# Four of seven Strassen products of a feed-forward layer accumulate in one PSUM bank, and the first tap of its convolution moves from VectorE to ScalarE

## The chip, the cores and the metric

One Trainium2 chip, one core. The metric is the device time of one execution in microseconds (us). The engines are named as the profile names them: PE is TensorE (PEld its weight loads), DVE is VectorE, ACT is ScalarE, POOL is GpSimd, SP is SyncE, whose queue issues the transfers. PE writes its sums to PSUM, which has eight banks; all other tiles lie in SBUF.

## The reference, cut to what matters

The program is a four-layer encoder over 528 tokens (16 of them fixed) of width 1024, in fp32. Each layer is a mixer (attention, RWKV, RG-LRU, attention), a layer norm, a gated feed-forward layer with a convolution over time, and a layer norm. Only the feed-forward layer is touched:

```python
def _dw_conv(x, w, b, pad_left):
    y = lax.conv_general_dilated(x, w[:, None, :], window_strides=(1,), ...)
    return y + b

def _conv_glu_ffn(x, w_in, conv_w, conv_b, w_out):
    g, u = jnp.split(x @ w_in, 2, axis=-1)          # w_in: 1024 x 5632
    g = _dw_conv(g, conv_w, conv_b, FFN_CONV_LEFT)  # 3 taps per channel
    return (jax.nn.silu(g) * u) @ w_out             # w_out: 2816 x 1024

for i in range(DEPTH):                              # 4 layers
    m = mixer_of_layer_i(h)
    h = _layer_norm(DN_ALPHA * h + m, ln_g[i, 0], ln_b[i, 0])
    f = _conv_glu_ffn(h, ffn_w_in[i], ffn_conv_w[i], ffn_conv_b[i], ffn_w_out[i])
    h = _layer_norm(DN_ALPHA * h + f, ln_g[i, 1], ln_b[i, 1])
```

## The kernel before

**Precision.** An fp32 matrix product is made of three matmuls on rounded parts: weight and operand are each split into a high part (`whi`, `xhi`; an ACT cast) and a rest (`wlo`, `xlo`; a DVE subtraction), and `mm3` adds hi*hi, hi*lo and lo*hi in one PSUM bank. A DVE split of a weight tile reads the raw weight and the high part and writes `wlo` (line 577, and line 411 for weights that are not Strassen's).

**Tiling.** `ffn` works through the 2816 channels in 11 steps `i` of 256 channels; each step has kind 0 (the gate g) and kind 1 (u). Step 0 is done with ordinary products. In steps 1 to 10 each (step, kind), called a *key* below, is a 2x2 block product by Strassen and Winograd's scheme: seven *products*, numbered 1 to 7, each of 12 matmuls of 264 columns (4 slices of the contraction times `mm3`), in place of eight. `products` makes the weight operands: it loads two raw tiles (`wraw`, `wraw2`), lets POOL form their sums (lines 586 to 591), and casts and splits the results in four pairs: for products 1 and 2, then 5 and 6, then 7 and 4, then 3. The operands of the activations (`thi`, `tlo`) are made once per layer by `operand_sums`.

**Combination.** `product(key, p)` runs one product into a bank of its own and then adds it to the outputs `c11`, `c12`, `c21`, `c22` (halves of two tiles `gp`) and to a helper tile `pu`. It runs the products in the order 1, 2, 6, 5, 7, 4, 3; product 1 is copied by ACT (line 642), and the rest take seven DVE adds (line 640).

**After a key.** For kind 0, each of the two `gp` tiles goes through the convolution: two POOL memsets of the edge columns, the first tap with the bias on DVE (line 696), two more taps on DVE (line 699), then Silu on ACT (line 701). For kind 1 DVE multiplies (line 705), and ACT and DVE split the result into `phi` and `plo` (lines 416, 417). From step 3 on, one *partial product* with `w_out` follows most keys (`partial`, 36 matmuls for three steps' channels, two DVE adds to `h` at line 511); its weights are split at line 411.

**Order.** The kernel's text gives each engine its work; a scheduler then fixes one static order per engine at build time, and an engine runs its own list strictly in that order. Buffers are few: four `whi` and four `wlo` tiles, three `wraw`, two `wraw2`, three `pu`, four `gp`, eight banks. The feed-forward layers are alike, so the program runs the stretch described here four times.

Of the kernel before, what the change touches and what calls it, by code (L numbers as in the profile page):

```python
# [11 lines left out]
AF = mybir.ActivationFunctionType  # L12
ALU = mybir.AluOpType
# [6 lines left out]
T = META + SEQ  # L20
HT = T // 2
# [7 lines left out]
KF = D_FF // 128  # L29
# [34 lines left out]
class Params:  # L64
# [6 lines left out]
    def add(self, name, size):  # L71
        self.at[name] = (self.n, size // 128)
        self.n += size // 128
# [252 lines left out]
class Kern:  # L326
# [89 lines left out]
        nc.scalar.copy(hi, src)  # L416
        nc.vector.tensor_tensor(out=lo, in0=src, in1=hi.bitcast(F32), op=ALU.subtract)

    def mm3(self, out, w, ws, x, xs, start, stop):

        nc = self.nc
        nc.tensor.matmul(out, lhsT=w[0][ws], rhs=x[0][xs], start=start, stop=False)  # L422
        nc.tensor.matmul(out, lhsT=w[0][ws], rhs=x[1][xs], start=False, stop=False)  # L423
        nc.tensor.matmul(out, lhsT=w[1][ws], rhs=x[0][xs], start=False, stop=stop)  # L424

    def lin(self, ps, pieces, x, halves):

# [166 lines left out]
    def ffn(self, l, split=True):  # L594
        nc, a = self.nc, self.a
        with ExitStack() as es:
            self.banks()
            fp = es.enter_context(self.tc.tile_pool(reuse_waits="tile", name=f"ffn{l}", bufs=1))
            K2 = KD // 2
# [21 lines left out]
            def begin(key):  # L621
                if key not in live:
                    L = live[key] = dict(gen=self.products(a["ffn_in"][l, key[0] * 2 + key[1]], 512, fp))
                    L["w"] = next(L["gen"])
                    L["t"] = [fp.tile([128, T + 2], F32, name="gp", tag="gp", bufs=4) for _ in range(2)]
                    L["c"] = [[t[:, 1 + j * HT:1 + j * HT + HT] for j in range(2)] for t in L["t"]]
                    L["u"] = [fp.tile([128, HT], F32, name="pu", tag="pu", bufs=3) for _ in range(2)]
                return live[key]

            def product(key, p):  # L630

                L = begin(key)
                if p not in L["w"]:
                    L["w"].update(next(L["gen"]))
                ps = self.bank()[:, :HT]
                for k in range(K2):
                    self.mm3(ps, L["w"][p], (slice(None), slice(k * 128, k * 128 + 128)), pairs[p], (slice(None), k), k == 0, k == K2 - 1)
                (c11, c12), (c21, c22) = L["c"]
                p1, u = L["u"]
                add = lambda out, x: nc.vector.tensor_tensor(out=out, in0=x, in1=ps, op=ALU.add)  # L640
                if p == 1:
                    nc.scalar.copy(p1, ps)
                elif p == 2:
                    add(c11, p1)
                elif p == 6:
                    add(c12, p1)
                elif p == 5:
                    add(u, c12)
                elif p == 7:
                    add(c21, c12)  # L650
                    add(c22, u)
                elif p == 4:
                    add(c21, c21)
                else:
                    add(c12, u)


# [8 lines left out]
                        self.late_apply() if q else self.late_stats()  # L666
            begin((1, 0))
            operand_sums()
            slots, queue = [], []

            def pieces(m, ch):
# [7 lines left out]
            for i in range(KF // 2):  # L679
                cs = []  # L680
                for kind in (0, 1):
                    key = (i, kind)
                    if i:
                        for p in (1, 2, 6, 5, 7, 4, 3):
                            product(key, p)
                        dst = live.pop(key)["t"]
                    else:
                        dst = first[kind]
                    for j in range(2):
                        f = 2 * i + j  # L690
                        if kind == 0:
# [1 line left out]
                            nc.gpsimd.memset(gp[:, 0:1], 0.0)  # L693
                            nc.gpsimd.memset(gp[:, T + 1:T + 2], 0.0)
                            c = fp.tile([128, T], F32, name="cv", tag="cv", bufs=2)
                            nc.vector.tensor_scalar(out=c, in0=gp[:, 0:T], scalar1=self.p(f"fc_w{l}0", f),
                                                    scalar2=self.p(f"fc_b{l}", f), op0=ALU.mult, op1=ALU.add)
                            for q in (1, 2):
                                nc.vector.scalar_tensor_tensor(out=c, in0=gp[:, q:q + T], scalar=self.p(f"fc_w{l}{q}", f), in1=c,  # L699
                                                               op0=ALU.mult, op1=ALU.add)  # L700
# [1204 lines left out]
```

## Time and profile before

| | |
|---|---|
| time of three runs, median (lowest, highest) | 3550.47 us (3542.97, 3557.28) |
| the profiled execution's own time | 3547.82 us |
| its span | 3546.0 us |
| mean granted PE clock | 0.966 of full speed |
| busy share of the span | PE 91%, PEld 87%, DVE 79%, ACT 45%, POOL 28% |
| chain of work that ended last | PE 59%, DVE 22%, ACT 8%, issue 5%, POOL 3%, DMA 2% |

A busy share says how long an engine had an instruction in it. A PE that is shown busy is not at its peak, since matmuls are pipelined and their ends are modelled. The chain is the work followed back from the last instruction, at each step to what released it. Where a stretch of one layer is shown, it is that of the first layer unless the line says otherwise; times are from the start of the span.

### The profile page before, as it was taken

The page shows a single profiled execution, that of the slowest core. Times are in us where ns is not written, and L with a number is a line of the kernel's source. Part 1 is how long each engine was busy: PE and PEld are TensorE (multiplying, and loading weights), DVE is VectorE, ACT ScalarE, POOL GpSimd, SP SyncE. Part 2 cuts the span into 40 slices and gives each one's busy share as a digit, 9 for nine tenths or more (in the row PEclk, how much of TensorE's full clock was granted, in tenths as well). Part 3 has the DMA queues.
Part 4 walks back from the last instruction along what each step waited for, and adds up shares of the span by engine and source line. Part 5 has one row for each costly group of instructions (what it writes and reads, how often), then busy time and mean ns, then how long its engine had stood idle before and what let it go on. Part 6 is the DMA issues. An engine that isn't in the chain of part 4 may idle for free.

```text
span 3546.0 us, 77810 instructions
## 1 busy us (share of the span) xinstructions
PE 3229.4 (91%) x31961; PEld 3099.3 (87%) x31961; DVE 2799.9 (79%) x5158; ACT 1610.5 (45%) x3035; POOL 1003.2 (28%) x1438
## 2 busy tenths in 40 slices
PE   5999889997988888878899988989999899989998
PEld 5899889996977877868899988979999799979998
DVE  5877799979436767657999779789997787789997
ACT  4765444333333333324333468643334666543433
POOL 0000253323006455434533200045431000045341
PEclk9999999998989999989999989999999999999999
DMA  2011213322422112122233222213332011212332
GB/s 82 22 40 38 75 63 103 103 84 86 136 77 48 35 38 45 25 53 88 82 105 97 87 72 72 79 54 100 98 94 81 20 37 34 66 43 93 103 92 71
DMA packets 155557, 250.06 MB, mean 71 GB/s; under 512 B 78496, under 2 KB 85824, under 8 KB 154944
## 3 DMA queue, kind: packets, MB, share of 16 engines
q1 hardware_dynamic: 155200, 245.08, 22.7%
q8 instruction: 251, 4.11, 0.5%
q14 instruction: 106, 0.87, 0.1%
HBM read 227.93 MB, written 17.10 MB: 69 GB/s over the span
## 4 chain that ended last, share of the span: by engine, by line
PE 59%; DVE 22%; ACT 8%; issue 5%; POOL 3%; DMA 2%; SPq 0%; DVEq 0%; ACTq 0%; POOLq 0%
PE bank L424 13%; PE bank L422 13%; PE bank L423 13%; PE pj L218 8%; PE ps L218 3%; DVE wlo L577 3%; PE s L218 3%; PE ch L218 1%; ACT wv L218 1%; PE rb L218 1%; DVE cv L699 1%; DVE pst L218 1%; DVE gp L640 1%; DVE cv L705 1%; DVE wlo L411 1%
## 5 line engine op out<-in xcount | busy, mean ns | idle before, releaser
L422 PE MATMUL bank<-xhi,whi 128*128 128x264 f32 x2144 | 608.3, 289 | 38.6 <-ACT xhi L416 28.9
L423 PE MATMUL bank<-xlo,whi 128*128 128x264 f32 x2144 | 618.3, 290 | 23.7 <-DVE xlo L564 12.5
L424 PE MATMUL bank<-xhi,wlo 128*128 128x264 f32 x2144 | 613.0, 289 | 23.4 <-DVE wlo L577 21.6
L422 PEld LDWEIGHTS bank<-xhi,whi 128*128 128x128 f32 x2144 | 406.3, 192 | 41.2 <-ACT xhi L416 28.8
L423 PEld LDWEIGHTS bank<-xlo,whi 128*128 128x128 f32 x2144 | 410.4, 191 | 33.1 <-DVE xlo L564 17.8
L424 PEld LDWEIGHTS bank<-xhi,wlo 128*128 128x128 f32 x2144 | 409.4, 192 | 29.7 <-DVE wlo L577 27.2
L424 PE MATMUL bank<-phi,wlo 128*128 128x264 f32 x1408 | 401.2, 285 | 2.1 <-DVE wlo L411 2.1
L422 PE MATMUL bank<-phi,whi 128*128 128x264 f32 x1408 | 400.5, 284 | 0.0
L423 PE MATMUL bank<-plo,whi 128*128 128x264 f32 x1408 | 400.3, 284 | 0.0
L576 ACT CAST whi<-wraw 128x1024 fp32r<-128x1024 f32 (+1 forms) x240 | 217.3, 907 | 263.9 <-PE bank L423 164.4
L577 DVE TENSOR_TENSOR wlo<-wraw,whi 128x1024 fp32r<-128x1024 f32 (+1 forms) x240 | 321.3, 1340 | 10.5 <-ACT whi L576 10.0
L411 DVE TENSOR_TENSOR wlo<-wraw,whi 128x1024 fp32r<-128x1024 f32 (+1 forms) x218 | 243.7, 1118 | 105.1 <-ACT whi L410 102.3
L410 ACT CAST whi<-wraw 128x1024 fp32r<-128x1024 f32 (+1 forms) x218 | 205.6, 946 | 198.8 <-PE bank L423 140.6
L424 PE MATMUL bank<-thi,wlo 128*128 128x264 f32 x960 | 276.2, 288 | 21.3 <-DVE wlo L577 21.3
L423 PE MATMUL bank<-tlo,whi 128*128 128x264 f32 x960 | 274.7, 286 | 0.0
L422 PE MATMUL bank<-thi,whi 128*128 128x264 f32 x960 | 273.9, 286 | 0.0
L424 PEld LDWEIGHTS bank<-phi,wlo 128*128 128x128 f32 x1408 | 264.8, 188 | 2.8 <-DVE wlo L411 2.8
L422 PEld LDWEIGHTS bank<-phi,whi 128*128 128x128 f32 x1408 | 265.1, 188 | 0.0
L423 PEld LDWEIGHTS bank<-plo,whi 128*128 128x128 f32 x1408 | 264.7, 188 | 0.0
L591 POOL TENSOR_TENSOR wraw<-wraw,wsum 128x512 f32<-128x512 f32 x80 | 113.4, 1418 | 384.7 <-DVE wlo L577 313.1
L424 PEld LDWEIGHTS bank<-thi,wlo 128*128 128x128 f32 x960 | 182.6, 190 | 23.8 <-DVE wlo L577 23.8
L422 PEld LDWEIGHTS bank<-thi,whi 128*128 128x128 f32 x960 | 182.9, 191 | 0.0
(402 smaller groups left out, 9841.1 us busy)
## 6 DMA issues: line engine op xcount, KB each, us to landing
wraw<-in_ffn_in_dram SPq DMA_DIRECT2D x176, 512.0 KB
wraw<-in_ffn_out_dram SPq DMA_DIRECT2D x96, 384.0 KB
wraw<-in_mla_o_dram SPq DMA_DIRECT2D x48, 256.0 KB
wraw<-in_rw_rkv_dram SPq DMA_DIRECT2D x24, 512.0 KB
wraw<-in_lru_in_dram SPq DMA_DIRECT2D x20, 512.0 KB
wraw<-in_mla_q_dram SPq DMA_DIRECT2D x16, 512.0 KB
wraw<-in_ffn_out_dram SPq DMA_DIRECT2D x16, 512.0 KB
rkv<-ro SPq DMA_DIRECT2D x24, 264.0 KB
```

The costliest lines, as they stand in the source:

```text
L218: op.fn(*op.args, **op.kw)
L410: nc.scalar.copy(hi[:, :cols], raw[:, :cols])
L411: nc.vector.tensor_tensor(out=lo[:, :cols], in0=raw[:, :cols], in1=hi[:, :cols].bitcast(F32), op=ALU.subtract)
L422: nc.tensor.matmul(out, lhsT=w[0][ws], rhs=x[0][xs], start=start, stop=False)
L423: nc.tensor.matmul(out, lhsT=w[0][ws], rhs=x[1][xs], start=False, stop=False)
L424: nc.tensor.matmul(out, lhsT=w[1][ws], rhs=x[0][xs], start=False, stop=stop)
L576: nc.scalar.copy(hi[:, cut], x[:, cut])
L577: nc.vector.tensor_tensor(out=lo[:, cut], in0=x[:, cut], in1=hi[:, cut].bitcast(F32), op=ALU.subtract)
L591: e.tensor_tensor(out=a1[:, 1], in0=a1[:, 1], in1=s[:, 1], op=ALU.subtract)
L640: add = lambda out, x: nc.vector.tensor_tensor(out=out, in0=x, in1=ps, op=ALU.add)
L699: nc.vector.scalar_tensor_tensor(out=c, in0=gp[:, q:q + T], scalar=self.p(f"fc_w{l}{q}", f), in1=c, op0=ALU.mult, op1=ALU.add)
L705: nc.vector.tensor_tensor(out=c, in0=c, in1=dst[j][:, 1:T + 1], op=ALU.mult)
```

## The change

Products 6, 7 and 4 accumulate in the bank in which product 1 of their key stands, and product 3 in the bank of product 5. Between them ACT copies the running sum out: after 6 to the helper tile `u` (products 1+6), after 7 to `c22` (1+6+7), after 4 to `c21` (1+6+7+4). DVE adds three times: `c11` = product 2 + copy of product 1, `c22` += bank of product 5, `c12` = bank of products 5+3 + `u`. So a key has three DVE adds and four ACT copies, where it had seven and one. Product 1 of the next key runs between products 7 and 4 of the present one, and its weights are prepared that much earlier. The convolution's first tap, with scale and bias per channel, is an ACT activation. The number of matmuls is the same.

```diff
-    def mm3(self, out, w, ws, x, xs, start, stop):
+    def mm3(self, out, w, ws, x, xs, start, stop, more=False):
...
-                ps = self.bank()[:, :HT]
+                if p in (1, 2, 5):
+                    L[p] = self.bank()[:, :HT]
+                on = {6: 1, 7: 1, 4: 1, 3: 5}.get(p, p)
+                ps = L[on]
                 for k in range(K2):
-                    self.mm3(ps, L["w"][p], (slice(None), slice(k * 128, k * 128 + 128)), pairs[p], (slice(None), k), k == 0, k == K2 - 1)
+                    self.mm3(ps, L["w"][p], (slice(None), slice(k * 128, k * 128 + 128)), pairs[p], (slice(None), k),
+                             k == 0 and on == p, k == K2 - 1, True)
...
                 elif p == 6:
-                    add(c12, p1)
-                elif p == 5:
-                    add(u, c12)
+                    nc.scalar.copy(u, ps)
                 elif p == 7:
-                    add(c21, c12)
-                    add(c22, u)
+                    nc.scalar.copy(c22, ps)
+                    nc.vector.tensor_tensor(out=c22, in0=c22, in1=L[5], op=ALU.add)
                 elif p == 4:
-                    add(c21, c21)
-                else:
+                    nc.scalar.copy(c21, ps)
+                elif p == 3:
                     add(c12, u)
...
             begin((1, 0))
             operand_sums()
+            product((1, 0), 1)
...
                     if i:
-                        for p in (1, 2, 6, 5, 7, 4, 3):
+                        for p in (2, 6, 5, 7):
+                            product(key, p)
+                        nxt = (i, 1) if kind == 0 else (i + 1, 0)
+                        if nxt[0] < KF // 2:
+                            product(nxt, 1)
+                        for p in (4, 3):
                             product(key, p)
...
-                            nc.vector.tensor_scalar(out=c, in0=gp[:, 0:T], scalar1=self.p(f"fc_w{l}0", f),
-                                                    scalar2=self.p(f"fc_b{l}", f), op0=ALU.mult, op1=ALU.add)
+                            nc.scalar.activation(out=c, in_=gp[:, 0:T], func=AF.Identity, scale=self.p(f"fc_w{l}0", f), bias=self.p(f"fc_b{l}", f))
```

What the change does to the engines' lists is shown at two places of the first layer. Numbers in names tell tiles apart and differ between the two programs.

**DVE, the second key (step 1, kind 1).** Line 640 is an add before; lines 645 and 654 are adds after; line 577 is a weight split. Before:

```order
L640 TENSOR_TENSOR gp_5364<-pu_5366,bank_5405 128x264
L577 TENSOR_TENSOR wlo_5497<-wraw_5494,whi_5496 128x1024
L640 TENSOR_TENSOR pu_5367<-gp_5364,bank_5419 128x264
L577 TENSOR_TENSOR wlo_5538<-wsum_5533,whi_5537 128x1024
L640 TENSOR_TENSOR gp_5365<-gp_5364,bank_5438 128x264
L640 TENSOR_TENSOR gp_5365<-pu_5367,bank_5438 128x264
L640 TENSOR_TENSOR gp_5365<-gp_5365,bank_5453 128x264
L577 TENSOR_TENSOR wlo_5571<-wraw2_5532,whi_5570 128x1024
L640 TENSOR_TENSOR gp_5364<-pu_5367,bank_5472 128x264
```

And in the changed kernel:

```order
L645 TENSOR_TENSOR gp_5314<-pu_5316,bank_5377 128x264
L577 TENSOR_TENSOR wlo_5484<-wraw_5308,whi_5483 128x512
L577 TENSOR_TENSOR wlo_5528<-wsum_5523,whi_5527 128x1024
L654 TENSOR_TENSOR gp_5315<-gp_5315,bank_5413 128x264
L577 TENSOR_TENSOR wlo_5559<-wraw2_5522,whi_5558 128x1024
L645 TENSOR_TENSOR gp_5314<-pu_5317,bank_5413 128x264
```

The last two adds read the bank of product 5 (`bank_5413`): line 654 before product 3 may add to it, line 645 after. One split stands between them.

**ACT, between product 4 of a kind-0 key and product 6 of the next (step 4 in the changed kernel, and the corresponding place of the program before).** Line 701 before and 709 after is Silu; line 576 a cast of Strassen weights, line 410 one of `w_out`; line 642 the copy of product 1. Before:

```order
L576 CAST whi_6440<-wraw_6330 128x512
L701 ACTIVATE cv_6272<-cv_6272 128x528
L701 ACTIVATE cv_6279<-cv_6279 128x528
L642 COPY pu_6338<-bank_6340 128x264
L410 CAST whi_6467<-wraw_6466 128x768
```

And in the changed kernel, where line 656 copies product 4's sum, 705 is the first tap and 651 the copy of product 6's sum:

```order
L576 CAST whi_6338<-wsum_6334 128x1024
L656 COPY gp_6034<-bank_6037 128x264
L576 CAST whi_6369<-wraw2_6333 128x1024
L705 ACTIVATE cv_6261<-gp_6033,par_64 128x528
L705 ACTIVATE cv_6268<-gp_6034,par_64 128x528
L709 ACTIVATE cv_6261<-cv_6261 128x528
L576 CAST whi_6389<-wraw_6387 128x1024
L709 ACTIVATE cv_6268<-cv_6268 128x528
L576 CAST whi_6425<-wraw_6204 128x512
L651 COPY pu_6213<-bank_6214 128x264
```

The last row is now followed by PE: product 7 adds to `bank_6214` and so comes after the copy. Ahead of it stand both Silus, which follow three and four DVE taps.

## Rows read from the trace of the kernel before

**Rows 1.** The page's busy times by engine: us (share of the span) xinstructions.

```profile
PE 3229.4 (91%) x31961; PEld 3099.3 (87%) x31961; DVE 2799.9 (79%) x5158; ACT 1610.5 (45%) x3035; POOL 1003.2 (28%) x1438
```

**Rows 2.** Busy time in stretches of layer 1 (three rows) and layer 3.

```profile
core 0: us, PE busy (x) PEld busy (x) DVE busy (x) ACT busy (x) POOL busy (x), PEclk, DMA share, GB/s
468.00:536.00 68.00, 55.55 (x422) 53.26 (x420) 66.07 (x82) 29.43 (x42) 37.59 (x33) 0.97 0.23 74
536.00:563.00 27.00, 26.26 (x211) 25.85 (x212) 26.77 (x36) 10.53 (x16) 12.35 (x12) 1.00 0.24 74
563.00:776.00 213.00, 213.00 (x1750) 213.00 (x1750) 195.09 (x275) 83.03 (x111) 76.56 (x73) 1.00 0.32 99
2366.00:2434.00 68.00, 57.80 (x422) 56.15 (x423) 67.08 (x84) 29.52 (x41) 37.65 (x33) 0.92 0.23 74
```

**Rows 3.** PE's groups in 466 to 563 us; the last columns are idle us and releasers.

```profile
L424 PE MATMUL bank<-xhi,wlo 128*128 128x264 f32 x114 | 33.2, 295 | 6.0 <-DVE wlo L577 6.0
...
L422 PE MATMUL bank<-xhi,whi 128*128 128x264 f32 x113 | 32.6, 289 | 0.8 <-ACT whi L576 0.8
L424 PE MATMUL bank<-thi,wlo 128*128 128x264 f32 x79 | 23.0, 293 | 5.3 <-DVE wlo L577 5.3
...
L424 PE MATMUL bank<-phi,wlo 128*128 128x264 f32 x24 | 6.9, 289 | 1.0 <-DVE wlo L411 1.0
```

**Rows 4.** The order of time on DVE in the first layer: start us, us.

```profile
473.48 0.56 DVE L696 TENSOR_SCALAR cv<-gp,par 128x528 f32<-128x528 f32 x1
473.95 1.21 DVE L577 TENSOR_TENSOR wlo<-wsum,whi 128x1024 fp32r<-128x1024 f32 x1
...
484.89 0.42 DVE L640 TENSOR_TENSOR gp<-gp,bank 128x264 f32<-128x264 f32 x1
485.23 0.42 DVE L640 TENSOR_TENSOR gp<-pu,bank 128x264 f32<-128x264 f32 x1
485.57 0.42 DVE L640 TENSOR_TENSOR gp<-gp,bank 128x264 f32<-128x264 f32 x1
...
487.39 1.99 DVE L696 TENSOR_SCALAR cv<-gp,par 128x528 f32<-128x528 f32 x2
489.30 2.79 DVE L699 SCALAR_TENSOR_TENSOR cv<-gp,par,cv 128x528 f32<-128x528 f32 x4
...
511.39 2.28 DVE L577 TENSOR_TENSOR wlo<-wsum,whi 128x1024 fp32r<-128x1024 f32 x1
```

**Rows 5.** The order of time on POOL, one instruction.

```profile
511.30 1.28 POOL L591 TENSOR_TENSOR wraw<-wraw,wsum 128x512 f32<-128x512 f32 x1 [3.37 <-DVE wlo L577]
```

**Rows 6.** ACT's groups in 563 to 776 us, and two of the whole span (cast, Identity).

```profile
L576 ACT CAST whi<-wraw 128x1024 fp32r<-128x1024 f32 x25 | 26.3, 1050 | 21.4 <-PE bank L423 8.9 <-PE bank L424 6.6 <-issue 4.0
...
L701 ACT ACTIVATE cv<-cv 128x528 f32<-128x528 f32 x14 | 9.1, 647 | 20.5 <-DVE cv L699 20.3
...
L576 ACT CAST whi<-wraw 128x512 fp32r<-128x512 f32 x13 | 8.1, 621 | 29.9 <-PE bank L423 26.7 <-POOL gp L694 3.3
L642 ACT COPY pu<-bank 128x264 f32<-128x264 f32 x13 | 4.8, 367 | 1.8 <-PE bank L424 1.8
...
L563 ACT CAST xhi<-h x96: 393/412/420, 430.8 to 3165.5; 128x264 fp32r<-128x264 f32 x96
L561 ACT ACTIVATE h<-h,par x96: 591/607/612, 430.2 to 3542.2; 128x264 f32<-128x264 f32 x96
```

**Rows 7.** DVE's groups in 563 to 776 us, and line 699 (min/median/max ns) over the span.

```profile
L577 DVE TENSOR_TENSOR wlo<-wraw,whi 128x1024 fp32r<-128x1024 f32 x26 | 42.5, 1636 | 2.5 <-ACT whi L576 2.4
...
L699 DVE SCALAR_TENSOR_TENSOR cv<-gp,par,cv 128x528 f32<-128x528 f32 x28 | 19.6, 757 | 0.0
...
L577 DVE TENSOR_TENSOR wlo<-wsum,whi 128x1024 fp32r<-128x1024 f32 x13 | 17.7, 1360 | 1.7 <-ACT whi L576 1.6
...
L699 DVE SCALAR_TENSOR_TENSOR cv<-gp,par,cv x176: 751/756/1798, 468.7 to 3470.6; 128x528 f32<-128x528 f32 x176
```

More of the change, by code (lines that the diff above doesn't have):

```diff
@@ L417, in split @@
         nc.vector.tensor_tensor(out=lo, in0=src, in1=hi.bitcast(F32), op=ALU.subtract)
-    def mm3(self, out, w, ws, x, xs, start, stop):
+    def mm3(self, out, w, ws, x, xs, start, stop, more=False):
         nc = self.nc
-        nc.tensor.matmul(out, lhsT=w[0][ws], rhs=x[0][xs], start=start, stop=False)
-        nc.tensor.matmul(out, lhsT=w[0][ws], rhs=x[1][xs], start=False, stop=False)
-        nc.tensor.matmul(out, lhsT=w[1][ws], rhs=x[0][xs], start=False, stop=stop)
+        nc.tensor.matmul(out, lhsT=w[0][ws], rhs=x[0][xs], start=start, stop=False, skip_group_check=more)
+        nc.tensor.matmul(out, lhsT=w[0][ws], rhs=x[1][xs], start=False, stop=False, skip_group_check=more)
+        nc.tensor.matmul(out, lhsT=w[1][ws], rhs=x[0][xs], start=False, stop=stop, skip_group_check=more)
     def lin(self, ps, pieces, x, halves):
```

## The prediction

> **What bounds the kernel now.** I read the page's engine shares first. PE leads with 91% and DVE is at 79% [rows 1], so a change that takes work from DVE can only pay where PE waits for DVE. I therefore cut a feed-forward layer into stretches. From 563 to 776 us PE is busy without a gap, 1750 matmuls in 213 us, which is one per 0.1217 us and 1.46 us for a product of 12; DVE is at 195 of 213 us there [rows 2]. Whatever DVE is relieved of in that stretch is worth nothing. From 468 to 536 us it is the other way round: DVE is busy for 66.07 of 68 us, PE for 55.55 us with 422 matmuls [rows 2]. At the full pitch these would take 422 x 0.1217 = 51.4 us, so 16.6 us are lost, and by the same sum 27 - 211 x 0.1217 = 1.3 us up to 563. The groups of PE say to whom: 6.0 + 5.3 us of idle time end with a weight split of DVE, 0.8 with a cast and 1.0 with the split for the first partial product [rows 3]; the rest is matmuls at a lower clock after the longest wait. In layer 3 the granted clock of the same stretch is 0.92 instead of 0.97, and its 422 matmuls still fill the same 68 us [rows 2]: DVE sets the length, not PE. So the ceiling of the change is about 17.9 us a layer, 72 us in all.
>
> **What the change takes from DVE, per layer, up to the first partial product.** By the order of the built programs DVE has 30 adds ahead of that product's weight split before, 13 after, and six first taps before, none after; and it has 21 Strassen splits after instead of 20, since product 1 of the next key has been pulled ahead.
>
> *Adds.* In a row of adds the starts lie 0.34 us apart (484.89, 485.23, 485.57 [rows 4]), so 17 adds are at most 5.8 us. They are not all net time. A split that starts 0.09 us after a POOL instruction of 1.28 us takes 2.28 us [rows 4, 5], another takes 1.21 us [rows 4]: DVE paid 1.07 us for POOL's 1.28 us. An add that runs while POOL works lets POOL go on, and without the add the next split pays. POOL is at work in 37.59 of the 68 us [rows 2], so 45% of 5.8 us, or 2.6 us, are sure. I take 4.0 us, near the middle, with 2.6 and 5.8 as bounds.
>
> *Taps.* A first tap costs 0.47 us where it stands alone (473.48 to 473.95) and 0.95 us in the pair from 487.39 to 489.30, which meets POOL [rows 4]. Six are 2.8 to 4.7 us by these two prices (two alone and four in pairs are 4.7). The extra would pass to the next DVE instruction, so I take 2.8.
>
> *Extra split, and product 1 ahead.* The split costs 1.21 to 2.28 us [rows 4]; in return PE has 1.46 us of work behind it when the first partial product begins. Net +0.2, between -0.8 and +0.3.
>
> *Later waits.* The 1.3 us lost between 536 and 563 us [rows 2] go if DVE is no longer late there: +0.9, between 0 and 1.3.
>
> **What it adds.** ACT gets three more copies a key at 0.367 us [rows 6] and 22 first taps a layer. The trace has no such activation on 528 columns: Silu on them takes 0.647 us, and Identity with scale and bias on 264 takes 0.607 us where a cast takes 0.412 [rows 6]. That makes 0.65 to about 0.83 us, an estimate from these rows. ACT is busy 29.43 of 68 us in the first stretch and 83.03 of 213 in the second [rows 2], so it has the room; the price is nothing unless order makes it one, and there are two such places.
>
> First, product 3 adds to the bank of product 5, so it waits for the DVE add at line 654, and the add of `c12` behind it on DVE waits for product 3: 12 x 0.1217 + 0.16 = 1.62 us (a matmul is shown 0.28 us long), while one split of 1.6 us [rows 7] stands between the two adds. DVE waits some 0.2 us in each of four or five keys: -1.0, between 0 (POOL uses the gap) and -2.0.
>
> Second, product 7 waits for the copy of product 6's sum, which on ACT stands behind two Silus, and these behind DVE's taps. For a key that follows a convolution in the stretch where PE is full, I count from the end of product 4: cast 1.05, split 1.36, the next split's start 0.34 later for the `c12` add and 1.6 for itself, three taps at 0.68 (2.79 us for four [rows 4]), Silu, cast, Silu and the cast of 512 columns at 0.1 less than their durations since they follow each other (0.55, 0.95, 0.55, 0.52), and the copy, 0.37 [rows 6, 7]. That is 9.3 us, and 0.2 for the hand-overs. PE arrives after 12 matmuls of product 3, 36 of the partial product, 36 of products 2, 6 and 5: 84 x 0.1217 = 10.2 us. Some 0.7 us are left. Now and then a split of 2.28 us eats them: -0.8 per layer over eight such steps, with nothing as the other bound of this case.
>
> **Sum.** 4.0 + 2.8 + 0.2 + 0.9 - 1.0 - 0.8 = 6.1 us a layer, 24 us in four layers. The bounds are 2.6 + 2.8 - 0.8 + 0 - 2.0 - 0.8 = 1.8, and 5.8 + 4.7 + 0.3 + 1.3 = 12.1 us a layer: 7 to 48 us. From the profiled execution's 3547.8 us this gives 3524 us. That execution was 2.7 us below the median of the runs shown, so for the median I say **3526 us**, and 3502 to 3543 as this case's own range.
>
> **Rivals.** *The port decides: next to nothing.* DVE's splits and POOL's sums take turns, as the split of 2.28 us beside POOL's 1.28 us shows [rows 4, 5], and a row of adds, each with one operand in PSUM, is the time in which POOL gets through. If every microsecond of POOL has to be paid somewhere, the adds give 0 and only 2.8 + 0.2 + 0.9 - 1.8 = 2.1 us a layer are left: 8 us, 3542 us. For it: POOL works in over half of the stretch. Against it: the four adds around 485 us run with POOL waiting, and go for good. The Trainium skill has the rule behind this in "SBUF — State Buffer", section "Who interferes with whom": DVE and GpSimd share one port pair as an exclusive lock, a DVE instruction with two SBUF inputs contends with a GpSimd instruction that reads SBUF, one with a single SBUF input does not. By that rule the removed adds are just the DVE work that never held POOL up, and the trace's two durations agree with it.
>
> *The copy is late: slower.* In the chain of the second place a split can take 2.28 instead of about 1.5 us and a tap 1.80 instead of 0.76 [rows 4, 7]. If both splits and one tap meet POOL in every step, the chain is 0.9 + 0.7 + 1.0 = 2.6 us longer, 1.9 us past the 0.7 that are left, and PE stands still at product 7 in eight steps of each of four layers: 32 x 1.9 = 61 us against 24 + 3 us of gain (the 0.8 a layer are in the 61), net 34 us, 3584 us. It decides from a mean delay of the chain of 1.5 us: 27 us over 32 steps are 0.8 us a step, and 0.7 us come before them. For it: PE has no gap at all there now, so any is new. Against it: DVE, now at 195 of 213 us, loses the adds and taps there and has more room.
>
> *All waits go.* If DVE's load falls below PE's from step 1 on, the whole 72 us go, less some of the first wait before any add is made: about 65 us, 3485 us. Against it: after the change DVE still has more work than PE in the steps without a partial product.
>
> **Numbers.** Likeliest case 0.56, port 0.20, late copy 0.16, all waits gone 0.08. A measurement of this kernel can tell about 0.5% from no change, which is 17.8 us: faster means below 3532.7 us. The likeliest case lies there four times in five (0.45), all waits gone always (0.08), the port case seldom (0.03): faster 0.56. Within 0.5% are the rest of the likeliest (0.11), most of the port case (0.17) and a late copy that only eats the gain (0.06): 0.34. Slower 0.10. The range reaches from between the likeliest's low end and the case of no waits to just past no change, 3498 to 3554 us, and leaves out the worst of the late copy and the best of the other end.
>
> **What would show it.** Right: the stretch from the first product to the first partial product shorter by 5 to 8 us in each layer, with DVE still nearly full and PE's waits still ending with line 577; the full stretch as long as before. Port: the same number of microseconds with splits that take longer on average. Late copy: PE idle ahead of `thi` matmuls at line 422, released by ACT's copy of `pu`, in the stretch that has no gap now. I am wrong if the time changes outside the feed-forward layers, or if ACT reloads tables between tap and Silu.

## The result, and the profile after

The changed kernel is slower: 3605.39 us as the median of four runs (3598.87 to 3610.61), against 3551.88 us for the kernel before. The ratio is 1.0157, with a 95% interval of 1.0137 to 1.0176. The prediction said 3526 us, with a range from 3498 to 3554.

These are the page's engine shares of the changed kernel; they answer to [rows 1].

```profile
PE 3247.2 (90%) x31961; PEld 3113.1 (86%) x31961; DVE 2696.0 (75%) x4750; ACT 1758.4 (49%) x3363; POOL 995.9 (28%) x1438
```

DVE has 408 instructions and 104 us less, as the change intended, and PE has as many matmuls as before. So DVE was relieved, and the time was lost elsewhere. To find where, I cut each layer at three matmuls that can be found in every variant: the first that reads `thi`, the first that reads `phi` (the first partial product), and the last that reads `thi`. Stretch A runs from the first to the second, stretch B from the second to the third. These are the windows of layer 1, of the kernel before and then of the changed one (the columns are those of [rows 2]):

```profile
471.60:534.78 63.18, 52.15 (x399) 50.26 (x397) 61.25 (x77) 25.12 (x36) 34.86 (x32) 0.97 0.24 75
534.78:772.41 237.63, 236.07 (x1934) 235.45 (x1932) 219.85 (x305) 92.57 (x125) 88.91 (x85) 1.00 0.31 97
```
```profile
473.62:538.41 64.79, 55.61 (x411) 53.25 (x409) 56.71 (x60) 36.76 (x58) 34.99 (x33) 0.95 0.25 82
538.41:788.07 249.66, 237.92 (x1925) 236.25 (x1924) 198.77 (x222) 118.28 (x182) 86.21 (x84) 0.99 0.29 90
```

A has 12 matmuls more after the change, because product 1 runs one key earlier. B has eight fewer (counted by their starts), and the tail from B's end to the last matmul that reads `phi` has four fewer. At 0.1217 us each these are 1.46, 0.97 and 0.49 us. As means over the four layers A went from 63.69 to 64.85 us, B from 237.05 to 249.75 us, and the tail from 49.74 to 49.27 us. Together this is 13.4 us a layer and 53.6 us in four layers; the medians differ by 53.5 us. In A, DVE is busy 4.5 us less and PE got nothing for it (0.3 us, if the 1.46 us are taken off). In B, where PE had hardly a gap, 12.7 us appeared, or 13.7 us for the same number of matmuls.

PE's groups in B of the changed kernel show one group with idle time:

```profile
L422 PE MATMUL bank<-thi,whi 128*128 128x264 f32 x180 | 52.2, 290 | 11.7 <-ACT pu L651 11.7
```

These are seven waits of 1.44 to 1.75 us, in seven of the eight keys that follow a convolution in B, each ended by ACT's copy of `pu`; the other layers have seven each too (1.41 to 2.02 us). This is what the prediction named as the sign of the late copy. The 11.7 us are the waits alone. The matmuls ran slower too: PE is shown busy for 237.92 us, where 1925 matmuls at 0.1217 us take 234.3, and the granted clock is 0.99 instead of 1.00.

One such wait, in the order of time, on PE, ACT, DVE and POOL (start us, us; in brackets idle us and what ended it):

```profile
609.31 0.29 PE L424 MATMUL bank<-thi,wlo 128*128 128x264 f32 x1
...
610.79 0.28 PE L424 MATMUL bank<-xhi,wlo 128*128 128x264 f32 x1
612.82 0.39 PE L422 MATMUL bank<-thi,whi 128*128 128x264 f32 x1 [1.75 <-ACT pu L651]
```
```profile
600.90 1.05 ACT L576 CAST whi<-wsum 128x1024 fp32r<-128x1024 f32 x1 [1.10 <-PE bank L424]
...
609.86 0.65 ACT L709 ACTIVATE cv<-cv 128x528 f32<-128x528 f32 x1 [4.73 <-DVE cv L707]
610.41 1.03 ACT L576 CAST whi<-wraw 128x1024 fp32r<-128x1024 f32 x1
611.35 0.64 ACT L709 ACTIVATE cv<-cv 128x528 f32<-128x528 f32 x1
611.89 0.60 ACT L576 CAST whi<-wraw 128x512 fp32r<-128x512 f32 x1
612.40 0.37 ACT L651 COPY pu<-bank 128x264 f32<-128x264 f32 x1
```
```profile
603.12 0.42 DVE L645 TENSOR_TENSOR gp<-pu,bank 128x264 f32<-128x264 f32 x1
603.46 2.25 DVE L577 TENSOR_TENSOR wlo<-wraw,whi 128x1024 fp32r<-128x1024 f32 x1
605.63 4.87 DVE L707 SCALAR_TENSOR_TENSOR cv<-gp,par,cv 128x528 f32<-128x528 f32 x4
```
```profile
603.34 1.29 POOL L586 TENSOR_TENSOR wsum<-wraw 128x512 f32<-128x512 f32 x1 [4.73 <-DMA wraw<-in_ffn_in_dram]
604.71 2.16 POOL L587 TENSOR_TENSOR wsum<-wsum,wraw 128x512 f32<-128x512 f32 x1
606.82 1.76 POOL L589 TENSOR_TENSOR wraw<-wraw,wraw 128x512 f32<-128x512 f32 x1
```

PE had finished product 6 at 609.60 (the first row) and product 5 at 611.07. The copy needs nothing else, but on ACT it stands behind two Silus, and the first Silu waits for DVE. DVE's split takes 2.25 us and its four taps 4.87 us; POOL's three sums of the next weights run from 603.34 to 608.58, right beside them. From the cast to the end of the copy it is 11.9 us, where the prediction had 9.3 us.

The eighth such key of the layer is the last one. There are no next weights to sum, POOL is silent, and PE does not wait (DVE, then ACT):

```profile
777.09 1.22 DVE L577 TENSOR_TENSOR wlo<-wraw,whi 128x1024 fp32r<-128x1024 f32 x1
778.23 2.80 DVE L707 SCALAR_TENSOR_TENSOR cv<-gp,par,cv 128x528 f32<-128x528 f32 x4
```
```profile
774.53 1.05 ACT L576 CAST whi<-wsum 128x1024 fp32r<-128x1024 f32 x1 [1.10 <-PE bank L424]
...
783.27 0.38 ACT L651 COPY pu<-bank 128x264 f32<-128x264 f32 x1 [0.45 <-PE bank L424]
```

From the cast to the end of the copy it is 9.1 us here, and the copy waits for PE.

The kernel before has the same meeting in the same place, but there it falls on other instructions (DVE, then POOL):

```profile
600.91 1.01 DVE L696 TENSOR_SCALAR cv<-gp,par 128x528 f32<-128x528 f32 x2
...
634.77 2.26 DVE L577 TENSOR_TENSOR wlo<-wraw,whi 128x1024 fp32r<-128x1024 f32 x1
636.95 2.97 DVE L696 TENSOR_SCALAR cv<-gp,par 128x528 f32<-128x528 f32 x2
```
```profile
634.65 1.29 POOL L586 TENSOR_TENSOR wsum<-wraw 128x512 f32<-128x512 f32 x1 [1.65 <-issue]
636.02 2.16 POOL L587 TENSOR_TENSOR wsum<-wsum,wraw 128x512 f32<-128x512 f32 x1
638.14 1.48 POOL L589 TENSOR_TENSOR wraw<-wraw,wraw 128x512 f32<-128x512 f32 x1
```

There the two first taps take the blow: 2.97 us, against 1.01 us for a pair at 600.91 with POOL silent. The second and third taps come after it and cost 0.76 us each [rows 7]. With the first taps gone to ACT, the second and third taps meet POOL.

In A of the changed kernel (473 to 539 us) PE's waits read so:

```profile
L422 PE MATMUL bank<-thi,whi 128*128 128x264 f32 x60 | 17.9, 298 | 4.6 <-ACT gp L653 3.0 <-ACT pu L651 1.5
L424 PE MATMUL bank<-thi,wlo 128*128 128x264 f32 x60 | 17.6, 294 | 4.4 <-DVE wlo L577 4.4
```

In [rows 3] nearly all of PE's idle time there ended with DVE's splits. Now half of it ends with ACT's copies, which stand behind Silus and `phi` casts. DVE, too, now waits for ACT in A:

```profile
L577 DVE TENSOR_TENSOR wlo<-wraw,whi 128x1024 fp32r<-128x1024 f32 (+1 forms) x15 | 19.3, 1303 | 6.9 <-ACT whi L576 6.9
```

With 1.1 us ahead of the splits of sums this is 8.0 us, where it was 1.9 us before. So DVE is no longer nearly full there, as the prediction had expected it to be (56.71 of 64.79 us). The clock does not explain A: over the four layers it is 0.97, 0.97, 0.92 and 0.92 before, and 0.95, 0.95, 0.95 and 0.97 after.

### The profile page after: what moved, and what is told of

Its sections match the earlier page's. It is cut to its first block, busy times and chain, and to the rows that moved or that the text cites. A ratio compares the mean times of both kernels' runs of the same rounds, so it can differ in the third digit from the quotient of the medians.

```text
span 3602.5 us, 77589 instructions
## 1 busy us (share of the span) xinstructions
PE 3247.2 (90%) x31961; PEld 3113.1 (86%) x31961; DVE 2696.0 (75%) x4750; ACT 1758.4 (49%) x3363; POOL 995.9 (28%) x1438
## 5 line engine op out<-in xcount | busy, mean ns | idle before, releaser
L423 PE MATMUL bank<-xlo,whi 128*128 128x264 f32 x2144 | 621.0, 291 | 23.8 <-DVE xlo L564 12.7
L577 DVE TENSOR_TENSOR wlo<-wraw,whi 128x1024 fp32r<-128x1024 f32 (+1 forms) x240 | 354.3, 1480 | 45.6 <-ACT whi L576 45.2
L411 DVE TENSOR_TENSOR wlo<-wraw,whi 128x1024 fp32r<-128x1024 f32 (+1 forms) x218 | 247.2, 1135 | 142.6 <-ACT whi L410 142.2
L586 POOL TENSOR_TENSOR wsum<-wraw 128x512 f32<-128x512 f32 x80 | 105.8, 1323 | 402.5 <-issue 291.0
L707 DVE SCALAR_TENSOR_TENSOR cv<-gp,par,cv 128x528 f32<-128x528 f32 x176 | 200.5, 1194 | 0.1
```

Source lines behind the costliest of these rows:

```text
L411: nc.vector.tensor_tensor(out=lo[:, :cols], in0=raw[:, :cols], in1=hi[:, :cols].bitcast(F32), op=ALU.subtract)
L577: nc.vector.tensor_tensor(out=lo[:, cut], in0=x[:, cut], in1=hi[:, cut].bitcast(F32), op=ALU.subtract)
L586: e.tensor_tensor(out=s[:, 0], in0=a2[:, 0], in1=a2[:, 1], op=ALU.add)
```

## The experiments

The theory (A in the expectations): the copies of the accumulating bank are late because of their place in ACT's queue, behind Silus that wait for DVE's taps, which POOL slows. The rivals: B, handing a bank from ACT back to PE costs this wherever the copy stands; C, the tap on ACT costs it; D, in the early stretch DVE with POOL beside it is the limit whatever ACT does.

| run | us (median) | ratio to before, 95% | A, mean us | B, mean us |
|---|---|---|---|---|
| the kernel before | 3551.9 | | 63.69 | 237.05 |
| the changed kernel | 3605.4 | 1.0157 (1.0137 to 1.0176) | 64.85 | 249.75 |
| silu_after | 3544.1 | 0.9969 (0.9958 to 0.9981) | 63.87 | 234.88 |
| no_pool | 3487.5 | 0.9813 (0.9798 to 0.9828) | 53.26 | 234.54 |
| tap_dve | 3606.3 | 1.0149 (1.0132 to 1.0166) | 66.29 | 247.48 |
| tap_alone | 3553.3 | 1.0000 (0.9990 to 1.0009) | 63.34 | 236.77 |
| copies_first | 3535.9 | 0.9953 (0.9940 to 0.9965) | 62.23 | 234.54 |
| split_first | 3540.3 | 0.9964 (0.9952 to 0.9976) | 61.73 | 234.54 |
| no_pool_before | 3493.6 | 0.9835 (0.9820 to 0.9849) | 52.91 | 235.26 |
| four_adds | 3548.1 | 0.9984 (0.9973 to 0.9995) | 65.35 | 234.62 |
| sums_dve | 3512.8 | 0.9885 (0.9870 to 0.9900) | 50.94 | 234.54 |
| before_sums_dve | 3554.9 | 1.0003 (0.9994 to 1.0012) | 58.29 | 238.93 |
| after_sums_dve | 3511.7 | 0.9888 (0.9864 to 0.9911) | 51.32 | 234.54 |
| sums_mix | 3507.3 | 0.9870 (0.9851 to 0.9889) | 55.32 | 234.54 |

Each ratio is to executions of the kernel before that were taken together with the run (medians 3551.9 to 3554.7 us). A and B are means over the four layers of one profiled execution. The rest of the program outside A, B and the tail behind them took 2133 to 2175 us in these executions; it differed by 15 us even between the kernel before and tap_alone, so small differences are better read from A and B. A and B can be compared directly where they hold the same matmuls. Counted by their starts, all forms with the change have 408 matmuls in A, the kernel before, tap_alone and no_pool_before 396, and before_sums_dve 366.

**silu_after: the order on ACT.** The convolution of a kind-0 key is written behind product 6 of the key after it, and an edge for the scheduler keeps its Silus behind that copy in ACT's queue. The orders of PE and POOL are those of the changed kernel; on DVE some adds of the partial products came to stand between the taps.

```diff
-                    nc.scalar.copy(u, ps)
+                    L["held"] = nc.scalar.copy(u, ps)
...
                         for p in (2, 6, 5, 7):
                             product(key, p)
+                            if p == 6 and late:
+                                late.pop()(live[key]["held"])
...
+                with self.tc.issue_after(held.ins) if held else ExitStack():
+                    for c in cv:
+                        nc.scalar.activation(out=c, in_=c, func=AF.Silu)
```

> The changed kernel with one difference: on ACT the two Silus of a kind-0 key are queued behind the copy of product 6 of the key after it (in the changed kernel they stand ahead of it). Adds, taps, banks and matmuls are the same. Theory A (the copy of product 6 is late because it stands behind two Silus that wait for DVE's taps): the seven waits of 1.65 to 1.75 us per layer ahead of product 7 go, about 7 x 1.7 = 12 us a layer, 48 us in all: 3550 to 3565, and no wait ahead of product 7 in the steady stretch is longer than 0.3 us. Theory B (handing a bank from ACT back to PE inside a sum costs this much wherever the copy stands): 3595 to 3610, the waits stay.

It took 3544.1 us, 6 us less than theory A's range, and faster than the kernel before. ACT, and below it PE's group in B:

```profile
601.17 0.38 ACT L651 COPY pu<-bank 128x264 f32<-128x264 f32 x1 [0.90 <-PE bank L424]
601.45 0.65 ACT L699 ACTIVATE cv<-cv 128x528 f32<-128x528 f32 x1
602.42 0.65 ACT L699 ACTIVATE cv<-cv 128x528 f32<-128x528 f32 x1 [0.33 <-DVE cv L694]
```
```profile
L422 PE MATMUL bank<-thi,whi 128*128 128x264 f32 x180 | 51.3, 285 | 0.0
```

The copy waits for PE alone, and the 11.7 us are gone, though taps still meet POOL (the one at 597.18 took 1.79 us). The hand-over itself costs nothing that shows: B is out. A fell by 1.0 us.

**no_pool: the weight sums left out.** The raw tiles stand in for the sums, so PE multiplies other weights; the order stays that of the changed kernel.

```diff
-        e = nc.gpsimd
-        e.tensor_tensor(out=s[:, 0], in0=a2[:, 0], in1=a2[:, 1], op=ALU.add)
...
-        yield dict(zip((5, 6), pair(s)))
+        yield dict(zip((5, 6), pair(a2)))
```

> The changed kernel without POOL's sums of the weight tiles (the raw tiles are used in their place, so the output is not the layer's); ACT's and DVE's order is as in the changed kernel. If the copy is late because taps and split on DVE are slowed while POOL works beside them (theory A with the port as the cause of the delay): the split goes back from 2.25 to about 1.2 us and the four taps from 4.9 to about 3 us, together 2.8 us earlier, more than the 1.7 us by which product 7 waits; the waits go and the time is 3540 to 3562. If the order on ACT alone makes the copy late, POOL or no POOL: waits of 1 us or more stay, 3585 to 3605.

3487.5 us. B has no waits left (234.54 us, as short as in any run), although the Silus still stand ahead of the copy, so the order makes the copy late only together with POOL. The same chain in this run (DVE, then ACT):

```profile
583.78 1.22 DVE L577 TENSOR_TENSOR wlo<-wraw,whi 128x1024 fp32r<-128x1024 f32 x1
584.91 2.80 DVE L702 SCALAR_TENSOR_TENSOR cv<-gp,par,cv 128x528 f32<-128x528 f32 x4
```
```profile
581.22 1.05 ACT L576 CAST whi<-wraw 128x1024 fp32r<-128x1024 f32 x1 [1.02 <-PE bank L423]
...
590.04 0.38 ACT L646 COPY pu<-bank 128x264 f32<-128x264 f32 x1 [0.34 <-PE bank L424]
```

It takes 9.2 us, within the 9.3 of the prediction, and the copy waits for PE. I had not expected the other 60 us: A fell by 11.6 us a layer, 46 us in all, and the rest of the program by 14 us.

**tap_dve and tap_alone: the tap by itself.** tap_dve is the changed kernel with line 705 as it was before (below); tap_alone is the kernel before with the reverse edit.

```diff
-                            nc.scalar.activation(out=c, in_=gp[:, 0:T], func=AF.Identity, scale=self.p(f"fc_w{l}0", f), bias=self.p(f"fc_b{l}", f))
+                            nc.vector.tensor_scalar(out=c, in0=gp[:, 0:T], scalar1=self.p(f"fc_w{l}0", f),
+                                                    scalar2=self.p(f"fc_b{l}", f), op0=ALU.mult, op1=ALU.add)
```

> The changed kernel with the convolution's first tap back on DVE; the accumulation and its copies stay. Theory A: the Silus now wait for six taps on DVE in place of one on ACT and two on DVE each; the copy of product 6 is later still by 0.7 to 1.6 us in each of some 28 steps: 3620 to 3650. Rival C (the tap on ACT costs the time): 3535 to 3560. Theory B: 3600 to 3610.

> The kernel before with only the first tap moved to ACT; all seven products keep banks of their own. Theories A and B: PE waits for no ACT copy inside a key, so a late Silu delays nothing: 3543 to 3556 (DVE has two operations fewer per kind-0 key). Rival C (the tap on ACT itself costs the time): 3590 to 3605.

Moving the tap changes nothing in either kernel's time. C is out. Theory A's number for tap_dve was wrong too, as the copy is no later there; that the time lies in the range of theory B, which silu_after has ruled out, is chance:

```profile
606.93 2.98 DVE L705 TENSOR_SCALAR cv<-gp,par 128x528 f32<-128x528 f32 x2
609.83 2.79 DVE L708 SCALAR_TENSOR_TENSOR cv<-gp,par,cv 128x528 f32<-128x528 f32 x4
```
```profile
607.91 1.05 ACT L576 CAST whi<-wraw 128x1024 fp32r<-128x1024 f32 x1 [3.30 <-PE bank L423]
611.98 0.65 ACT L710 ACTIVATE cv<-cv 128x528 f32<-128x528 f32 x1 [3.01 <-DVE cv L708]
```

Six taps take 5.77 us where four took 4.87, because the first two catch POOL again; and the cast of 1.05 us that stood between the Silus now stands ahead of them, in time in which ACT waits anyway. In A of layer 1, DVE's taps of the kernel before and of tap_alone show the same exchange:

```profile
L699 DVE SCALAR_TENSOR_TENSOR cv<-gp,par,cv 128x528 f32<-128x528 f32 x11 | 8.9, 848 | 0.0
...
L696 DVE TENSOR_SCALAR cv<-gp,par 128x528 f32<-128x528 f32 x5 | 4.5, 935 | 0.0
```
```profile
L698 DVE SCALAR_TENSOR_TENSOR cv<-gp,par,cv 128x528 f32<-128x528 f32 x12 | 13.7, 1189 | 0.0
```

Before it is 13.4 us for 16 taps, after it is 13.7 us for 12. DVE as a whole is busy no less in this stretch, 62.46 us with 73 instructions against 61.25 us with 77:

```profile
475.64:539.59 63.95, 53.02 (x398) 51.44 (x397) 62.46 (x73) 30.56 (x43) 32.85 (x32) 0.95 0.24 74
```

**copies_first: all copies ahead.** The edit is shown against silu_after: the Silus stand behind the next key's copy of product 7, and a kind-1 key's multiplication and `phi` split are written behind the next key's product 6, with the casts behind its copy.

```diff
+            def glu(i, dst, cs, held=None):
+                slots.append([fp.tile([128, 2, T], F32R, name=n, tag=n, bufs=6) for n in ("phi", "plo")])
+                for j in range(2):
+                    nc.vector.tensor_tensor(out=cs[j], in0=cs[j], in1=dst[j][:, 1:T + 1], op=ALU.mult)
+                    with self.tc.issue_after(held.ins) if held else ExitStack():
+                        self.split(slots[i][0][:, j], slots[i][1][:, j], cs[j])
...
-                            if p == 6 and late:
-                                late.pop()(live[key]["held"])
+                            if late and p == (6 if late[0][0] else 7):
+                                late.pop()[1](live[key]["held"])
```

> The kernel of the run silu_after with the same done for the steps without partial products: the Silus of a kind-0 key stand behind the next key's copy of product 7 (c22), and the multiplication, phi and plo of a kind-1 key are issued with the phi casts behind the next key's copy of product 6. Theory A for the early stretch (the gain of fewer adds went into waits for ACT's copies that stand behind Silus and phi casts): the five waits of silu_after's first layer that end with such a copy (0.89, 1.33, 0.37, 1.13 and 0.37 us, 4.1 us together) go; the stretch from the first Strassen matmul to the first partial product falls from 62.7 to 64.8 us to about 59 to 60.5 us; 4 x 4 = 16 us: 3528 (3522 to 3536). Rival D (DVE with POOL beside it is the limit there, and the next split is as late as the copy was): waits of L577 take their place, 3539 to 3547.

3535.9 us, at the upper end of theory A's range. PE's idle time in A (477 to 540 us):

```profile
L422 PE MATMUL bank<-xhi,whi 128*128 128x264 f32 x78 | 23.4, 300 | 2.6 <-DVE gp L654 2.6
...
L424 PE MATMUL bank<-thi,wlo 128*128 128x264 f32 x60 | 18.0, 300 | 4.9 <-DVE wlo L577 4.9
```

ACT's copies have left the list, and product 3's wait for line 654, which the prediction had priced at 1.0 us, took part of their place. The waits for line 577 did not shrink (4.4 us in the same group of silu_after), which is the sign of rival D. A is 1.6 us shorter than in silu_after, not the 4 us expected.

**split_first: DVE's order at the start.** copies_first, with step 0's convolution behind product 6 of key (1,0), its taps behind that product's split on DVE.

```diff
+                    with ExitStack() if i else self.tc.issue_after(self.cut.ins):
...
-                            if late and p == (6 if late[0][0] else 7):
-                                late.pop()[1](live[key]["held"])
+                            while late and p == (6 if late[-1][0] else 7):
+                                late.pop(0)[1](live[key]["held"])
...
-                    if not i and kind == 0 or i == KF // 2 - 1:
+                    if i == KF // 2 - 1:
```

> copies_first, and at the start of a layer's Strassen products DVE's taps of step 0 are queued behind the split of the weight sums of key (1,0), which product 6 waits for; step 0's Silus and phi casts go behind the first copy of product 6. In silu_after that split waits for three taps that take 3.29 us beside POOL; product 6 waits 3.63 us for it and PE's clock is at half for about 10 us after. Theory A with the queue's order as cause there too: the wait of 3.6 us shrinks to 0.5 us or less, with 3 to 8 us per layer gained according to what the clock does: 3497 to 3520. Rival D: the split of product 7's weights, which follows the taps now, is late by as much: within 5 us of copies_first.

3540.3 us, and A's mean moved by 0.5 us, as rival D has it. The wait moved: product 6 waits 1.80 us where it waited 2.51 in copies_first, and product 7 waits 3.47 us where it waited 2.35. The group has 5.3 us for line 577 where it had 4.9:

```profile
L424 PE MATMUL bank<-thi,wlo 128*128 128x264 f32 x60 | 17.9, 298 | 5.3 <-DVE wlo L577 5.3
```

**no_pool_before: the control.** The same cut as no_pool, in the kernel before.

> The kernel before without POOL's sums of the weight tiles (the raw tiles in their place, so the output is not the layer's). If the accumulating banks save the DVE time that the prediction counted (17 adds of 0.34 us per layer ahead of the first partial product) wherever nothing else is late, the run is slower than no_pool's 3487.5 by up to 4 x 5.8 = 23 us: 3495 to 3512. If with POOL silent DVE is no limit any more, in either form: 3484 to 3493.

3493.6 us, between the two. With POOL silent, the change is worth 6 us by the medians, whose intervals overlap, and 3.4 us by A, B and the tail. Leaving the sums out also spares DVE's splits the wait for them, but that is not where the time went. DVE's busy time in A fell from 61.25 us to 50.81 us though the stretch has eight DVE instructions more, so the instructions themselves became shorter.

**four_adds: the adds put back.** copies_first, with four adds per key in steps 1 and 2 into a spare tile.

```diff
                 elif p == 3:
                     add(c12, u)
+                if key[0] < 3 and p in (2, 5, 3):
+                    for _ in range(1 + (p == 5)):
+                        add(spare, p1)
```

> copies_first with four more DVE adds per key in steps 1 and 2 (into a spare tile, in the form of the add of product 2, spread over products 2, 5 and 3): about as many as the accumulation took away in the stretch ahead of the first partial product. If those adds bound that stretch, as the first term of the prediction's sum says (0.34 us each): 16 x 0.34 = 5.4 us per layer, 22 us in all: 3550 to 3560. If they lay in DVE's slack, or beside other waits: 3533 to 3543.

12 us more than copies_first, between the two expectations: A grew by 3.1 us a layer, 0.2 us for each add of 0.34.

**sums_dve, before_sums_dve, after_sums_dve: the sums on DVE.** One line, in copies_first, in the kernel before and in the changed kernel:

```diff
-        e = nc.gpsimd
+        e = nc.vector
```

> copies_first with the four sums of weight tiles per key on DVE in place of POOL. Theory (DVE is slowed while POOL works beside it, and this bounds the early stretch): DVE was busy 40.9 us there in the run without the sums; with 4 keys' 16 sums of about 0.68 us (a split of as many columns in that run) 51.8 us, against 56.4 us in copies_first and the 52.9 us that the stretch lasted without the sums. The stretch falls from 62 to 53 to 57 us: 3487 + 0 to 20 us: 3488 to 3512. Rival (the sums, now in DVE's queue, wait there for their transfers and hold up the splits behind them): 3530 or more.

> The kernel before with the sums of weight tiles on DVE. By the same count DVE has 50.8 us (the kernel before without the sums) + 10.9 = 61.7 us ahead of the first partial product, where it has 61.3 us now: no gain there, 3540 to 3560. If the time is near that of sums_dve instead, the accumulation has no part in what the move gives.

> The changed kernel, with its own order on ACT, and the sums of weight tiles on DVE in place of POOL. If the copy of product 6 is late because DVE's split and taps ahead of the Silus are slowed beside POOL (2.25 and 4.87 us; 1.22 and 2.8 us without it), the chain is 3.1 us shorter and the sums put 0.7 to 2.7 us back into DVE's queue: the waits of 1.7 us ahead of product 7 shrink to 0 to 1 us, 3512 to 3535. If the order on ACT alone makes the copy late: 3545 or more.

3512.8, 3554.9 and 3511.7 us: just above the expected range, inside it, and just below it. The windows A and B of layer 1, of after_sums_dve and then of before_sums_dve:

```profile
479.92:531.99 52.07, 51.55 (x408) 51.34 (x409) 49.47 (x73) 33.88 (x54) 0.53 (x8) 0.97 0.33 103
531.99:766.53 234.54, 234.54 (x1926) 234.34 (x1924) 181.71 (x278) 120.74 (x182) 1.85 (x28) 1.00 0.32 96
```
```profile
478.42:536.31 57.89, 50.05 (x369) 48.15 (x367) 54.91 (x92) 24.19 (x34) 0.67 (x10) 0.94 0.23 72
536.31:775.27 238.96, 238.96 (x1963) 238.96 (x1962) 215.93 (x362) 95.63 (x125) 1.87 (x28) 1.00 0.32 99
```

With the change and the sums on DVE, PE is busy 51.55 of 52.07 us in A and without a gap in B, and DVE has room (49.47 us). The order on ACT no longer matters: after_sums_dve keeps the changed kernel's order and is as fast as sums_dve. In the kernel before, DVE is busy 54.91 us in A and PE waits. A is 5.4 us shorter there too and B 1.9 us longer, but the first partial product comes earlier in this program's order, so that 30 matmuls (3.65 us) have passed from A to B. For the same work each of the two is 1.8 us shorter. These 14 us in four layers were lost again outside: the rest of the program took 20.7 us more in its profiled execution. With the change it took 16 us more (after_sums_dve against the changed kernel) and 18 us more (sums_dve against copies_first), but A, B and the tail gained 115 and 45 us there.

DVE's groups in A of after_sums_dve carry the price:

```profile
L707 DVE SCALAR_TENSOR_TENSOR cv<-gp,par,cv 128x528 f32<-128x528 f32 x8 | 5.6, 764 | 0.0
...
L586 DVE TENSOR_TENSOR wsum<-wraw 128x512 f32<-128x512 f32 x5 | 3.4, 689 | 0.1
```

A sum costs DVE 0.69 us. A tap costs 0.76 us again, where the changed kernel had a mean of 1.11 us in A.

**sums_mix: the first key's sums back on POOL.**

```diff
-    def products(self, src, n, pool):
+    def products(self, src, n, pool, e):
...
-        e = nc.gpsimd
...
-                    L = live[key] = dict(gen=self.products(a["ffn_in"][l, key[0] * 2 + key[1]], 512, fp))
+                    L = live[key] = dict(gen=self.products(a["ffn_in"][l, key[0] * 2 + key[1]], 512, fp, nc.gpsimd if key == (1, 0) else nc.vector))
```

> sums_dve with the sums of key (1,0) alone back on POOL; they lie in the stretch of the layer norm ahead, where DVE's queue is full. In sums_dve that stretch (from the last partial product of a layer to the next layer's first Strassen matmul, layers 2 to 4) is 5.7, 3.3 and 7.2 us longer than in copies_first. If the first key's sums in DVE's queue are the cause: 4 x 3 to 7 us back, less 1 to 3 us per layer for the first splits beside POOL: 3490 to 3508. If not: 3508 to 3520.

3507.3 us, the lowest of the runs that keep the sums, but its interval overlaps those of sums_dve and after_sums_dve. A is 4.4 us a layer longer and the rest of the program 21.6 us shorter than in sums_dve: given and taken in nearly equal parts. The time lies at the upper end of the range that the expectation gave for its cause.

## Why the prediction was wrong, point by point

Between the forecast of 6.1 us gained a layer and the 13.4 us lost lie 19.5 us. For the same number of matmuls, 13.8 of them are in B and 5.7 in A.

**The failed step: the price of the copy of product 6.** The prediction had 9.3 us for the chain and 0.2 for the hand-overs, 0.7 us to spare, and so -0.8 us a layer. It is 11.9 us. The failure is in two durations: the second split took 2.17 us up to the next start where 1.6 was put, and the time from the first tap to the first Silu was 4.23 us where three taps at 0.68 were put. Both come from one cause. The prediction priced each instruction by its typical row in the kernel before, and the taps by rows with POOL silent, while POOL's sums come in this very place in seven of the eight such keys. Where POOL is silent, in the eighth key and in no_pool, the chain stays within the 9.3 us (9.1 and 9.2, with the copy waiting for PE at its end). The trace of before showed the meeting, but in layer 1 on the two first taps, which the change took away. A place's price was taken for an instruction's price. What it cost is 12.7 us a layer in B (13.7 for the same number of matmuls) instead of 0.8, and silu_after, which changes the copy's place, gave back 14.9.

**The rival was right in place and sign.** "The copy is late" put the waits at product 7 and had 1.9 us for each of 32, 61 us; there are 28 of about 1.7, 47 us. The 59 us that silu_after gave back in B are near its 61, but in part by luck, since slower matmuls, which it had not counted, make up the difference. It came out at 3584 us instead of 3605 because it set 24 + 3 us of gain against them, which the changed kernel did not have. What the prediction held against it, more room on DVE in the full stretch, was there (219.85 us busy in B of layer 1 before, 198.77 after) and did not help: the delay is made in single places, not by the average load.

**Adds, +4.0 us a layer.** Nearly right in size where the copies are on time: four_adds prices 16 of them at 3.1 us, inside the bounds. But the changed kernel could not cash it. In A the waits for DVE's splits became waits for ACT's copies of 4.6 us; copies_first, without these, has an A that is 2.9 us shorter than before, the 1.46 us of product 1 taken off.

**Taps, +2.8 us a layer.** Zero: 0.35 us in A, and 1.0000 (0.9990 to 1.0009) for the whole in tap_alone. The prediction said that POOL's share passes to the next DVE instruction and counted 0.47 us as sure. DVE's taps took 13.4 us before and 13.7 us without the first ones. The instructions that came in their place paid all of it.

**Later waits, +0.9.** B in copies_first is 234.54 us; with the 0.97 us of eight matmuls added it is 1.5 us shorter than before. The waits went as forecast; the gain is a little above the bound of 1.3.

**Product 3 and line 654, -1.0.** 0.2 us in layer 1 of the changed kernel, where the other waits come first, but 2.6 us in layer 1 of copies_first, past the bound of 2.0.

**The extra split and product 1 ahead, +0.2.** This was not tried by itself.

**The port rival** was half right. That each microsecond of POOL has to be paid somewhere held for the taps, but there the rival had left the prediction's 2.8 us standing; the adds, which it set at 0, gave 0.2 us each in four_adds. What was held against it, the adds around 485 us, says nothing: POOL stands idle for 6.69 us up to 487.69 us and is released by nothing that the profile shows. The Trainium skill's rule in "SBUF — State Buffer", section "Who interferes with whom", makes an exception that the prediction left out: `tensor_scalar`, with its one SBUF input, can take the shared ports too, in a mode that uses two ports, when its operands allow that. The trace agrees: a pair of first taps took 2.97 us beside POOL and 1.01 us without.

**Where the gain was.** The ceiling of 17.9 us a layer was nearly real: sums_dve reaches 15.8 of it in A and B, for the same number of matmuls. But POOL's sums beside DVE held it, more than the number of adds. Without the sums, A falls to 53 us in the kernel before as in the changed one. With the sums on DVE, where they take 0.69 us each, the change is worth 43 us: 3511.7 us with it and 3554.9 us without.

## What to carry to other kernels

When a change makes PE wait for a copy, price the whole queue ahead of that copy at the place where it will run, with what the other engines do there, and not by the median of each instruction; if the instruction that met the other engine is taken away, its neighbour meets it next. Count a saving on an engine that runs slower beside another one (2.25 instead of 1.22 us for a split here) as sure only if the other engine's work goes too. Two changes that are each worth nothing or less (fewer adds, 1.0157; sums on DVE, 1.0003) can be worth 1.1% together (0.9888), so try a change again once its limit has been moved.

## What the runs showed of the hardware

POOL's time beside DVE was worth more than its busy share tells: 35 us of POOL work in A cost PE 10.8 us a layer in the kernel before, by which A became shorter when it was left out. The same sum takes 1.29 us or more on POOL and 0.69 us on DVE. The same four taps took 4.87 us beside POOL's sums and 2.80 us without them. An accumulating bank that ACT reads between two products cost PE nothing that shows when the copy was on time: in B of copies_first PE is busy for all of the 234.54 us, at one matmul per 0.122 us.
